# Weight matrices stored in DRAM block by block instead of as plain rows: a hybrid flow-matching step on one Trainium2 core

## The chip, the core and the metric

The kernel runs on one core of one Trainium2 chip. The metric is the device time of one execution in microseconds (us). Data live in DRAM (the chip's HBM) and are moved by the core's 16 DMA engines into the on-chip memory, SBUF, which has 128 partitions; matmul results land in PSUM. Five engines work side by side, each through its own instructions in a fixed order: TensorE (PE, whose weight loads are shown as PEld), VectorE (DVE), ScalarE (ACT), GpSimd (POOL) and SyncE (SP), which here only issues DMAs. An engine that meets an instruction whose semaphore has not come stands still, and with it all that is queued behind it.

## The reference, cut to what matters

One layer of a hybrid backbone is computed for 2048 latent tokens and 128 context tokens (2176 rows of 1024 channels, float32):

```python
xn   = rmsnorm(h, ln_g) * (1 + scale) + shift            # scale, shift, gate: silu(cond) @ w_ada + b_ada
proj = xn @ w_in                                         # (1024, 7696)
qkv, beta, dec, z_a, u_b, v_b, z_b, x_c, z_c, gates = split(proj)
o_a  = rmsnorm(delta_bidir(conv(qkv), decay, beta, state)) * silu(z_a)   # chunked gated DeltaNet, both directions
o_b  = chunk_sgu(u_b, v_b) * silu(z_b)                   # spatial gating in chunks of 128 tokens
o_c  = fourier_mix(x_c) * silu(z_c)
pb   = [o_a @ w_branch[0], o_b @ w_branch[1], o_c @ w_branch[2]]         # each (512, 1024)
merged = sum(sigmoid(gates[n]) * pb[n] for n in range(3))
y    = rmsnorm(h + gate * (merged @ w_out), final_g)     # w_out (1024, 1024)
```

The outputs are `y` for both token groups and the final DeltaNet states of the context tokens.

## The kernel before, in words

**Numbers.** Each float32 operand of a large product is split into two float16 parts, a high one (`hi`) and a low one (`lo`), scaled by a power of two; a product is three float16 matmuls, hi by hi, hi by lo and lo by hi. The normalised input is held whole in SBUF as `xh` and `xl`.

**Weights.** They come in blocks of 128 output columns. The list `wlist` (line 255) holds 84 entries in the order of use: 36 column blocks of `w_in` for the branches (4 for z_a, 12 for q, k and v of the DeltaNet, 4 for v_b, 16 for u_b, z_b, x_c and z_c), and then, for each branch in the order 1, 2, 0 and each of the 8 blocks of the merge, a block of `w_in` for the gate and a block of `w_branch`. The 8 blocks of `w_out` are read by `out_w` (line 1443) during the last merge. A block goes through these steps:

- `read_w` (line 198): SP issues one DMA into `wst`, a float32 tile with two buffers; contraction row k·128+p of the block goes to partition p, place k. So a partition gets 8 runs (4 for `w_branch`) of 128 floats, 512 bytes each, from rows that lie a whole matrix row apart in DRAM.
- `converting` (line 203): ACT squares the block and sums it (line 214, the square is written to the `lo` tile and thrown away), DVE makes the bound `wscb` (line 180), PE adds it over partitions, DVE takes from it the scale (lines 188 to 192), ACT writes `hi` (line 223), and DVE writes `lo` (line 224). That last step sets the `wst` buffer free for the next read.

`weight_step` does one of these steps at a time, called by `pace.tick` between the pieces of the main work, so that the conversion of coming weights is spread over it. The tiles' names tell the blocks apart: `zhi`/`zlo` for z_a, `v4hi`/`v4lo` for v_b, `bhi`/`blo` for `w_branch`, `wohi`/`wolo` for `w_out`, `whi`/`wlo` for the others.

**Stages.** First the modulation: 16 DMAs of `w_ada` into `ast`, matmuls and vector sums, results turned through `adr` (line 414). The first two weight blocks are read just behind the last `ast` load (line 437, `issue_after`). Then the input is normalised, and z_a, q, k and v are projected (the conv result is stored by POOL as `qkv`). From then on a generator, `delta()`, is woven into the main work in small steps: preparation of the DeltaNet's chunks, then the scan, 17 chunks forward and 17 backward, a chain of small matmuls with ACT and DVE steps between them (lines 908, 909, 980, 1002, 1019), its operands loaded by SP from DRAM (`skn`, `sv`, `sk`, `sq`, `sqk`, `sn`, `ES`, `N`). The main work beside it is the spatial gating, the Fourier mixing and then `merge` (line 1356), three times over 8 blocks: gate product, sigmoid, branch product with the operand `big` (read back through `st`, line 1351), their product added to a row `mrow`, which from the second pass on is loaded by SP (line 1371), added to by POOL and stored again by POOL's queue (`mrg`, line 1400). The last stage multiplies by `w_out`, adds the residual and normalises.

**Order.** The kernel is built with a scheduler that fixes each engine's order when the program is made. All loads named above, the weights' and the scan's, stand in SP's one queue (q1 in the profile), in that order; ACT issues some stores on its own queue (q10) and POOL on another (q0).

Of the kernel before, what the change touches and what calls it, by code (L numbers as in the profile page):

```python
# [20 lines left out]
P = 128  # L21
D = 1024
KT = 8
# [5 lines left out]
WB = 512  # L29
EPS = 1e-6  # L30
C_QKV, C_BD, C_ZA, C_U, C_V, C_ZB, C_XC, C_ZC, C_G = 0, 1536, 1552, 2064, 2576, 3088, 3600, 4112, 4624
# [25 lines left out]
def _const_array():  # L57
    i = np.arange(P)
    out = {}
    out["ident"] = np.eye(P)  # L60
    out["ones"] = np.ones((P, P))
    le = i[:, None] <= i[None, :]
    ge = i[:, None] >= i[None, :]
    out["tri_f"] = le * 1.0
    out["tri_b"] = ge * 1.0
    out["neg_f"] = np.where(le, 0.0, -3e4)
    out["neg_b"] = np.where(ge, 0.0, -3e4)
    b64, b32 = i // 64, i // 32
    a2 = np.arange(2)[None, :]
    out["m1f"] = (b32[:, None] == 2 * a2 + 1) * 1.0  # L70
    out["m1b"] = (b32[:, None] == 2 * a2) * 1.0
    out["m2f"] = (b64 == 1)[:, None] * 1.0
    out["m2b"] = (b64 == 0)[:, None] * 1.0
    out["bm"] = (b32[:, None] == np.arange(4)[None, :]) * 1.0
    c = np.arange(64)
    planes = [("c", 32) if (kd, k) == ("s", 0) else (kd, k) for q in range(0, 32, 8) for kd in "cs" for k in range(q, q + 8)]
    f = np.zeros((64, 64))
    for n_, (kind, k) in enumerate(planes):
        ang = 2 * np.pi * (c * k % 64) / 64
        f[:, n_] = (np.cos(ang) if kind == "c" else np.sin(ang)) / 8.0  # L80
    d2 = np.zeros((P, 2, 64))
    for r in range(2):
        d2[r * 64:(r + 1) * 64, r, :] = f
    out["dft2"] = d2.reshape(P, P)
    ang = 2 * np.pi * (i[:, None] * i[None, :] % P) / P
    C128, S128 = np.cos(ang) / math.sqrt(P), np.sin(ang) / math.sqrt(P)
    out["dftcs"] = np.concatenate([C128, S128], 1)
    out["dftms"] = -S128
    out["dfth"] = np.concatenate([C128[:, 0:65], S128[:, 1:64]], 1)
    r = np.arange(32)  # L90
    ang = 2 * np.pi * (r[:, None] * r[None, :] % 32) / 32
    C32, S32 = np.cos(ang) / math.sqrt(32), np.sin(ang) / math.sqrt(32)

    def bd(ms):
        m = np.zeros((P, P))
        for n_, x in enumerate(ms):
            m[n_ * 32:(n_ + 1) * 32, n_ * 32:(n_ + 1) * 32] = x
        return m

    out["rc"] = bd([C32] * 4)  # L100
    out["rms"] = bd([-S32] * 4)
    out["rmc"] = bd([-C32] * 4)
    out["rxa"] = bd([C32, -S32, -S32, -S32])
    out["rxb"] = bd([-S32, -C32, -C32, -C32])
    c32 = np.ascontiguousarray(np.concatenate([out[n_] for n_, _ in _CONSTS], 1).astype(np.float32))
    four = c32[:, _CF:] * np.float32(CS)
    hi = four.astype(np.float16)
    lo = (four - hi.astype(np.float32)).astype(np.float16)
    return np.ascontiguousarray(c32[:, 0:_CF]), np.ascontiguousarray(np.stack([hi, lo], 1))


class _W:
    pass


@with_exitstack
def hybrid_flow_kernel(ctx: ExitStack, tc: tile.TileContext, x_prompt, x_sample, state_delta, c, c_ctx, ln_g, w_ada,
                       b_ada, w_in, conv_w, a_log, dt_bias, o_norm_g, sgu_norm_g, w_spatial, b_spatial, w_branch,
                       w_out, final_g, consts, consts16, y_prompt, y_sample, new_state, dbg=None):
    nc = tc.nc  # L120
    V, A, G, PE, SY = nc.vector, nc.scalar, nc.gpsimd, nc.tensor, nc.sync
    uid, rot = [0], [0]
# [8 lines left out]
    def sb(pl, shape, tag, dt=F32, bufs=None):  # L131
        kw = {} if bufs is None else {"bufs": bufs}
        return pl.tile(list(shape), dt, tag=tag, name=nm(tag), **kw)
# [61 lines left out]
    def load_w(src, nkt, cols=P, hi=None, lo=None, tag="w", bufs=5):  # L195
        return convert(read_w(src, nkt, cols, tag), nkt, cols, hi, lo, tag, bufs)

    def read_w(src, nkt, cols=P, tag="w"):
        st = sb(wp, [P, nkt, cols], "wst" if cols == P else tag + "st", bufs=2 if cols == P else 1)
        SY.dma_start(st, src.rearrange("(k p) c -> p k c", p=P))  # L200
        return st

    def converting(w, st, nkt, cols=P, hi=None, lo=None, tag="w", bufs=5):
# [22 lines left out]
    def convert(st, nkt, *args, **kw):  # L226
        w = _W()
        for _ in converting(w, st, nkt, *args, **kw):
            pass
        return w  # L230
# [15 lines left out]
            mm(ps, lh[:, k, :], w.lo[:, k, c0:c0 + n], False, False)  # L246
            mm(ps, ll[:, k, :], w.hi[:, k, c0:c0 + n], False, k == nkt - 1)

    w_in_, w_ada_, b_ada_ = w_in[0], w_ada[0], b_ada[0]
    xs_, xp_ = x_sample[0], x_prompt[0]  # L250

    def xrows(t0, n):
        return xs_[t0:t0 + n, :] if t0 < NS else xp_[t0 - NS:t0 - NS + n, :]

    wlist = []
    for c0 in [C_ZA + g * P for g in range(4)]:
        wlist.append((w_in_[:, c0:c0 + P], KT, "z", 4))
    for c0 in ([C_QKV + i * P for i in range(12)] + [C_V + g * P for g in range(4)]
               + [x_ + g * P for g in range(4) for x_ in (C_U, C_ZB)] + [x_ + g * P for g in range(4) for x_ in (C_XC, C_ZC)]):
        wlist.append((w_in_[:, c0:c0 + P], KT, "v" if C_V <= c0 < C_V + WB else "w", 4))  # L260
    for n in (1, 2, 0):
        for db in range(KT):
            wlist.append((w_in_[:, C_G + n * D + db * P:C_G + n * D + (db + 1) * P], KT, "w", 4))
            wlist.append((w_branch[0, n][:, db * P:(db + 1) * P], 4, "b", 2))
    v4, vfilled = [], [0]
    goal = [0]
    wdone, wnext, wread, wlate, bwp, wsteps = [], [0], [], [0], [], []
# [1 line left out]
    def read_next():  # L269
        if len(wread) < min(len(wdone) - len(wsteps) + 2, len(wlist)):  # L270
            src, nkt, tag, bufs = wlist[len(wread)]
            wread.append(read_w(src, nkt))
# [26 lines left out]
    def getw(n=1, ahead=0):  # L299
        i = wnext[0]  # L300
        wnext[0] += n
        fetch(i + n)
        while len(wdone) - len(wsteps) < i + n:
            weight_step()
        fetch(i + n + ahead)
        r = wdone[i:i + n]
        return r[0] if n == 1 else r
# [84 lines left out]
    def load_x(t0, tn):  # L392
        xt = sb(p0p, [P, tn // P, D], "xt")
        SY.dma_start(xt, xrows(t0, tn).rearrange("(j p) d -> p j d", p=P))
        xts[t0] = xt

    for blk in range(8):
# [4 lines left out]
        for k0 in range(0, KT, 4):  # L402
            st = sb(p0p, [P, 4, 256], "ast", bufs=8)
# [31 lines left out]
    with tc.issue_after(last_ada.ins):  # L435
        read_next()
        read_next()
        load_x(*TBS[1])
        zaw = getw(4)
        bdp = sb(wp, [P, KT, 32], "bdp", F16, bufs=1)  # L440
        bdw = load_w(w_in_[:, C_BD:C_BD + 16], KT, 16, hi=bdp[:, :, 0:16], lo=bdp[:, :, 16:32], tag="d")
    szlate = []
    for ti, (t0, tn) in enumerate(TBS):
        if t0 not in xts:
            load_x(t0, tn)
        g = 0 if t0 < NS else 1
# [164 lines left out]
    for ct in range(12):  # L611
        w = getw(1, 2 if ct < 6 else min(4, 15 - ct))
# [292 lines left out]
    pair = lambda t_, h: (t_[:, 0, hs(h)], t_[:, 1, hs(h)])  # L905
# [301 lines left out]
    for g in range(4):  # L1207
# [5 lines left out]
        for ti, (t0, tn) in enumerate(TBS):  # L1213
            st = vrow[:, t0:t0 + tn]
# [224 lines left out]
    whi = sb(orp, [P, KT, D], "wohi", F16)  # L1439
    wlo = sb(orp, [P, KT, D], "wolo", F16)  # L1440
    winv = sb(orp, [P, KT], "winv8")

    def out_w(i):
        w = load_w(w_out[0][:, i * P:(i + 1) * P], KT, hi=whi[:, :, i * P:(i + 1) * P], lo=wlo[:, :, i * P:(i + 1) * P])
        V.tensor_mul(winv[:, i:i + 1], w.inv, sx)

    turn = []
# [42 lines left out]
    def tail(db):  # L1490
        out_w(db)
        if db == KT - 1:
            for _ in gates:
                pass
# [12 lines left out]
    for i_, t in enumerate(order):  # L1507
# [39 lines left out]
            SY.dma_start(out, hh)  # L1547


_INS = ['x_prompt', 'x_sample', 'state_delta', 'c', 'c_ctx', 'ln_g', 'w_ada', 'b_ada', 'w_in', 'conv_w', 'a_log',  # L1550
        'dt_bias', 'o_norm_g', 'sgu_norm_g', 'w_spatial', 'b_spatial', 'w_branch', 'w_out', 'final_g']
_OUTS = [((1, NP, D), 'float32'), ((1, NS, D), 'float32'), ((1, 1, 2, H, P, P), 'float32')]


# [21 lines left out]
```

## Time and profile before

| | |
|---|---|
| time, three runs | 2195.5, 2200.12, 2200.22 us; median 2200.12 |
| the profiled execution | 2197.38 us, its span 2195.6 us |
| granted TensorE clock, mean | 0.991 |
| busy: PE, PEld, DVE, ACT, POOL | 2122.4, 1218.2, 1311.2, 1013.1, 737.1 us |
| DMA queue q1 (SP) | 251690 packets, 267.38 MB, 40.5% of 16 engines' time |
| weight loads | 60 blocks of `w_in` of 512 KB, 24 of `w_branch` of 256 KB, 8 of `w_out` of 512 KB, one of 16 columns (`dst`) |

How to read it: the span is from the first to the last instruction, and 1.8 us of the profiled execution lie around it. Busy times of different engines overlap. An engine's row in a timeline ends in brackets with the time for which the engine stood idle before it and what ended that; an arrow in a group reads "written tile <- read tiles". "DMA share" is the mean busy share of the 16 DMA engines, and a packet is one contiguous run that one of them moves.

### The profile page before, as it was taken

To read this page: it belongs to the slowest core of one execution; us is meant where nothing else is said; L and a number is where in the kernel's file an instruction comes from. 1 tells how busy PE (TensorE), PEld (TensorE's weight loads), DVE (VectorE), ACT (ScalarE), POOL (GpSimd) and SP (SyncE) were. 2 spreads that over 40 slices of the span, in tenths; PEclk is the share of its full clock that TensorE was granted. 3 is DMA by queue.
4 is the path that set the end of the run, shared out by engine and by line. 5 is a ranking of instruction groups with operands and counts; after the bars stand their busy time and mean duration, and the time that the engine had idled before them with its cause. 6 is when DMAs were issued, how large, how long until landed. Compare 5 with 4: busy or idle time off the path is not lost.

```text
span 2195.6 us, 42626 instructions
## 1 busy us (share of the span) xinstructions
PE 2122.4 (97%) x16258; PEld 1218.2 (55%) x16258; DVE 1311.2 (60%) x3141; ACT 1013.1 (46%) x2345; POOL 737.1 (34%) x893
## 2 busy tenths in 40 slices
PE   7999999999999999899899999999999999999998
PEld 3565444455455577777455555555655444444444
DVE  5736845479878697466655555755574544233454
ACT  3544644355555674444544445655553422222332
POOL 1421533223334332443321223345442222122553
PEclk9999999999999999999999999999999999999999
DMA  8434733167777754434645556766665544333542
GB/s 282 143 96 146 266 114 110 61 208 219 239 224 238 213 167 107 119 118 143 217 155 166 167 161 187 239 195 206 204 200 154 166 125 129 119 101 109 183 151 106
DMA packets 304280, 365.11 MB, mean 166 GB/s; under 512 B 39393, under 2 KB 215754, under 8 KB 302026
## 3 DMA queue, kind: packets, MB, share of 16 engines
q1 hardware_dynamic: 251690, 267.38, 40.5%
q0 software_dynamic: 12688, 51.27, 6.5%
q10 hardware_dynamic: 39696, 43.72, 5.9%
q8 instruction: 128, 2.10, 0.4%
q14 instruction: 78, 0.64, 0.1%
HBM read 234.67 MB, written 127.62 MB: 165 GB/s over the span
## 4 chain that ended last, share of the span: by engine, by line
PE 45%; DVE 8%; DMA 7%; ACT 3%; issue 2%; POOL 1%; ACTq 0%; SPq 0%; POOLq 0%; DVEq 0%
PE b L166 45%; DMA st<-br 1%; DMA wst<-in_w_in_dram 1%; DVE XB L792 1%; DVE E L793 1%; DMA ei<-XB 1%; DMA wst<-in_w_branch_dram 1%; DMA sv<-kv 1%; DMA mt<-mrg 1%; DVE wlo L224 1%; DVE o L925 0%; DMA mrg<-mrow 0%; ACT nd L745 0%; DVE sv L980 0%; DVE big L1354 0%
## 5 line engine op out<-in xcount | busy, mean ns | idle before, releaser
L166 PE MATMUL b<-xh,whi 128*128 128x512 f16 (+1 forms) x1920 | 650.2, 347 | 7.4 <-DVE sg L1130 3.4
L166 PE MATMUL b<-xl,whi 128*128 128x512 f16 (+1 forms) x1920 | 650.6, 347 | 0.0
L166 PE MATMUL b<-xh,wlo 128*128 128x512 f16 (+1 forms) x1920 | 649.8, 347 | 0.0
L166 PEld LDWEIGHTS <-whi 128*128 128x128 f16 x3904 | 356.7, 98 | 339.6 <-issue 15.8
L166 PEld LDWEIGHTS <-wlo 128*128 128x128 f16 x1952 | 191.1, 98 | 177.9 <-issue 1.5
L166 PE MATMUL b<-big,bhi 128*128 128x512 f16 (+1 forms) x960 | 251.7, 348 | 5.8 <-ACT big L1353 5.4
L1393 POOL TENSOR_TENSOR mrow<-mrow,sg 128x512 f32<-128x512 f32 (+1 forms) x80 | 96.0, 1201 | 289.0 <-DVE sg L1392 158.5
L166 PE MATMUL b<-big,blo 128*128 128x512 f16 (+1 forms) x480 | 163.7, 348 | 0.0
L1383 ACT ACTIVATE sg<-b,winv 128x512 f32<-128x512 f32 (+1 forms) x120 | 74.1, 618 | 154.0 <-PE b L166 153.6
L166 PEld LDWEIGHTS <-xh 128*128 128x128 f16 x1496 | 118.7, 99 | 35.0 <-DVE yT L1306 3.9
L633 POOL TENSOR_TENSOR cy<-cy,raw 128x545 f32<-128x545 f32 (+1 forms) x48 | 76.6, 1623 | 180.3 <-ACT raw L632 180.3
L166 PEld LDWEIGHTS <-bhi 128*128 128x128 f16 x960 | 87.2, 98 | 77.0 <-ACT big L1353 1.6
L180 DVE CAST wscb<-wss 128x1 bf16<-128x1 f32 x93 | 14.3, 154 | 192.4 <-ACT wlo L214 79.4
L1392 DVE SCALAR_TENSOR_TENSOR sg<-b,binv,sg 128x512 f32<-128x512 f32 (+1 forms) x80 | 53.5, 668 | 101.2 <-PE b L166 91.1
L166 PE MATMUL b<-whi,xh 128*128 128x128 f16 x544 | 95.2, 222 | 5.2 <-DVE yT L1306 3.7
L166 PE MATMUL b<-wlo,xh 128*128 128x128 f16 x544 | 95.2, 222 | 0.0
L166 PE MATMUL b<-whi,xl 128*128 128x128 f16 x544 | 95.1, 222 | 0.0
L166 PE MATMUL b<-wohi,mh 128*128 128x512 f16 (+2 forms) x248 | 91.9, 372 | 1.5 <-ACT mh L1463 1.5
L865 POOL COPY T<-ES 32x256 f16<-32x256 f16 x68 | 28.7, 422 | 191.5 <-DMA ES<-ei 178.2
L166 PE MATMUL b<-wohi,ml 128*128 128x512 f16 (+2 forms) x248 | 91.7, 372 | 0.3 <-DVE ml L1464 0.3
L166 PE MATMUL b<-wolo,mh 128*128 128x512 f16 (+2 forms) x248 | 91.9, 372 | 0.0
L224 DVE SCALAR_TENSOR_TENSOR wlo<-wst,wsc,whi 128x1024 f16<-128x1024 f32 x52 | 72.6, 1399 | 31.2 <-ACT whi L223 30.4
(458 smaller groups left out, 4305.2 us busy)
## 6 DMA issues: line engine op xcount, KB each, us to landing
wst<-in_w_in_dram SPq DMA_DIRECT2D x60, 512.0 KB, 5.9
qkv<-cy POOLq DMA_DIRECT2D x12, 1089.0 KB, 5.2
st<-br SPq DMA_DIRECT2D x48, 256.0 KB, 4.5
mrow<-mrg SPq DMA_DIRECT2D x18, 512.0 KB, 3.5
mrow<-mrg SPq DMA_DIRECT2D x16, 576.0 KB, 3.8
mrg<-mrow POOLq DMA_DIRECT2D x16, 576.0 KB, 3.8
dc<-dec SPq DMA_DIRECT2D x17, 512.0 KB
kq<-qkv SPq DMA_DIRECT2D x34, 256.0 KB, 5.1
```

Source lines behind the costliest of these rows:

```text
L166: PE.matmul(out, l, r, start=start, stop=stop)
L180: V.tensor_copy(sb16, ss)
L224: V.scalar_tensor_tensor(w.lo, st, s, w.hi, ALU.mult, ALU.subtract)
L633: G.tensor_tensor(y[:, c0:c1], y[:, c0:c1], raw[:, 1 + c0:1 + c1], ALU.mult)
L792: V.tensor_tensor(t3, X3[:, 0:k, k:k + 1].to_broadcast([P, k, n_]), E3[:, k:k + 1, k:32].to_broadcast([P, k, n_]), ALU.mult)
L793: V.tensor_tensor(E3[:, 0:k, k:32], E3[:, 0:k, k:32], t3, ALU.subtract)
L865: G.tensor_copy(T16[rows(a0, b), :, :, b], ES[0:32, :, 2 * a0 + b, :, wT])
L1383: A.activation(sg, ps, AF.Sigmoid, scale=gw.inv)
L1392: V.scalar_tensor_tensor(sg, ps, binv[:, 1:2], sg, ALU.mult, ALU.mult)
L1393: G.tensor_tensor(mr, mr, sg, ALU.add)
```

## The change

The weights are laid out anew before the launch, on the host: for each block of 128 columns, partition p's 8 (or 4) runs of 128 floats stand side by side, and the blocks stand one behind the other. A block is then 128 rows of 4 KB (2 KB for `w_branch`), 512 KB (256 KB) in one piece; the 16 columns for beta and decay become 128 rows of 512 bytes. The kernel reads each block with one DMA as before, of the same size, into the same tile. Nothing else in the kernel's text is changed.

```diff
+def _by_block(w, starts, width=P):
+    w = np.asarray(w)
+    return np.ascontiguousarray(np.stack([w[:, c0:c0 + width].reshape(-1, P, width).transpose(1, 0, 2).reshape(P, -1) for c0 in starts]))
+
+def _laid_out(inputs):
+    w_in, w_branch, w_out = [np.asarray(inputs[n_])[0] for n_ in ("w_in", "w_branch", "w_out")]
+    cols = [db * P for db in range(KT)]
+    return {
+        "w_blk": _by_block(w_in, [c0 + i * P for c0, i in _blocks()]),
+        "w_bd": _by_block(w_in, [C_BD], 16)[0],
+        "w_brb": np.stack([_by_block(w_branch[n], cols) for n in range(3)]),
+        "w_outb": _by_block(w_out, cols),
+    }
...
     def read_w(src, nkt, cols=P, tag="w"):
         st = sb(wp, [P, nkt, cols], "wst" if cols == P else tag + "st", bufs=2 if cols == P else 1)
-        SY.dma_start(st, src.rearrange("(k p) c -> p k c", p=P))
+        SY.dma_start(st, src.rearrange("p (k c) -> p k c", c=cols))
         return st
...
-    for c0 in [C_ZA + g * P for g in range(4)]:
-        wlist.append((w_in_[:, c0:c0 + P], KT, "z", 4))
...
-    for n in (1, 2, 0):
-        for db in range(KT):
-            wlist.append((w_in_[:, C_G + n * D + db * P:C_G + n * D + (db + 1) * P], KT, "w", 4))
-            wlist.append((w_branch[0, n][:, db * P:(db + 1) * P], 4, "b", 2))
+    for i, (n_, g) in enumerate(_blocks()):
+        wlist.append((w_blk[i], KT, "z" if n_ == C_ZA else "v" if n_ == C_V else "w", 4))
+        if n_ >= C_G:
+            wlist.append((w_brb[(n_ - C_G) // D, g], 4, "b", 2))
...
-        w = load_w(w_out[0][:, i * P:(i + 1) * P], KT, hi=whi[:, :, i * P:(i + 1) * P], lo=wlo[:, :, i * P:(i + 1) * P])
+        w = load_w(w_outb[i], KT, hi=whi[:, :, i * P:(i + 1) * P], lo=wlo[:, :, i * P:(i + 1) * P])
```

`_blocks()` lists the 60 blocks of `w_in` in the order of `wlist`. The load of the 16 columns reads `w_bd` in the same way.

More of the change, by code (lines that the diff above doesn't have):

```diff
@@ L109, in _const_array, with _blocks @@
     return np.ascontiguousarray(c32[:, 0:_CF]), np.ascontiguousarray(np.stack([hi, lo], 1))
+def _blocks():
+    parts = [(C_ZA, g) for g in range(4)] + [(C_QKV, i) for i in range(12)] + [(C_V, g) for g in range(4)]
+    for pair in ((C_U, C_ZB), (C_XC, C_ZC)):
+        parts += [(x_, g) for g in range(4) for x_ in pair]
+    return parts + [(C_G + n * D, db) for n in (1, 2, 0) for db in range(KT)]
+def _by_block(w, starts, width=P):
[10 more added lines that the diff above has]
+    }
 class _W:
@@ L117, in hybrid_flow_kernel @@
 def hybrid_flow_kernel(ctx: ExitStack, tc: tile.TileContext, x_prompt, x_sample, state_delta, c, c_ctx, ln_g, w_ada,
-                       b_ada, w_in, conv_w, a_log, dt_bias, o_norm_g, sgu_norm_g, w_spatial, b_spatial, w_branch,
-                       w_out, final_g, consts, consts16, y_prompt, y_sample, new_state, dbg=None):
+                       b_ada, w_blk, w_bd, conv_w, a_log, dt_bias, o_norm_g, sgu_norm_g, w_spatial, b_spatial, w_brb,
+                       w_outb, final_g, consts, consts16, y_prompt, y_sample, new_state, dbg=None):
     nc = tc.nc
@@ L247, in gemm_N @@
             mm(ps, ll[:, k, :], w.hi[:, k, c0:c0 + n], False, k == nkt - 1)
-    w_in_, w_ada_, b_ada_ = w_in[0], w_ada[0], b_ada[0]
+    w_ada_, b_ada_ = w_ada[0], b_ada[0]
     xs_, xp_ = x_sample[0], x_prompt[0]
@@ L255, in hybrid_flow_kernel @@
     wlist = []
-    for c0 in [C_ZA + g * P for g in range(4)]:
-        wlist.append((w_in_[:, c0:c0 + P], KT, "z", 4))
-    for c0 in ([C_QKV + i * P for i in range(12)] + [C_V + g * P for g in range(4)]
-               + [x_ + g * P for g in range(4) for x_ in (C_U, C_ZB)] + [x_ + g * P for g in range(4) for x_ in (C_XC, C_ZC)]):
-        wlist.append((w_in_[:, c0:c0 + P], KT, "v" if C_V <= c0 < C_V + WB else "w", 4))
-    for n in (1, 2, 0):
-        for db in range(KT):
-            wlist.append((w_in_[:, C_G + n * D + db * P:C_G + n * D + (db + 1) * P], KT, "w", 4))
-            wlist.append((w_branch[0, n][:, db * P:(db + 1) * P], 4, "b", 2))
+    for i, (n_, g) in enumerate(_blocks()):
+        wlist.append((w_blk[i], KT, "z" if n_ == C_ZA else "v" if n_ == C_V else "w", 4))
+        if n_ >= C_G:
+            wlist.append((w_brb[(n_ - C_G) // D, g], 4, "b", 2))
     v4, vfilled = [], [0]
@@ L440, in hybrid_flow_kernel @@
         bdp = sb(wp, [P, KT, 32], "bdp", F16, bufs=1)
-        bdw = load_w(w_in_[:, C_BD:C_BD + 16], KT, 16, hi=bdp[:, :, 0:16], lo=bdp[:, :, 16:32], tag="d")
+        bdw = load_w(w_bd, KT, 16, hi=bdp[:, :, 0:16], lo=bdp[:, :, 16:32], tag="d")
     szlate = []
@@ L1547, in hybrid_flow_kernel @@
             SY.dma_start(out, hh)
-_INS = ['x_prompt', 'x_sample', 'state_delta', 'c', 'c_ctx', 'ln_g', 'w_ada', 'b_ada', 'w_in', 'conv_w', 'a_log',
-        'dt_bias', 'o_norm_g', 'sgu_norm_g', 'w_spatial', 'b_spatial', 'w_branch', 'w_out', 'final_g']
+_INS = ['x_prompt', 'x_sample', 'state_delta', 'c', 'c_ctx', 'ln_g', 'w_ada', 'b_ada', 'w_blk', 'w_bd', 'conv_w', 'a_log',
+        'dt_bias', 'o_norm_g', 'sgu_norm_g', 'w_spatial', 'b_spatial', 'w_brb', 'w_outb', 'final_g']
 _OUTS = [((1, NP, D), 'float32'), ((1, NS, D), 'float32'), ((1, 1, 2, H, P, P), 'float32')]
@@ L1563 @@
     arrays, args = {}, []
-    fixed = dict(zip(("consts", "consts16"), _const_array()))
+    fixed = dict(zip(("consts", "consts16"), _const_array()), **_laid_out(inputs))
     for name in _INS + ["consts", "consts16"]:
```

## The prediction, written before the changed kernel was run

> **What bounds the kernel now.** I read the page first, for who is busy and what chain ended last.
>
> ```profile
> PE 2122.4 (97%) x16258; PEld 1218.2 (55%) x16258; DVE 1311.2 (60%) x3141; ACT 1013.1 (46%) x2345; POOL 737.1 (34%) x893
> DMA packets 304280, 365.11 MB, mean 166 GB/s; under 512 B 39393, under 2 KB 215754, under 8 KB 302026
> PE b L166 45%; DMA st<-br 1%; DMA wst<-in_w_in_dram 1%; DVE XB L792 1%; DVE E L793 1%; DMA ei<-XB 1%; DMA wst<-in_w_branch_dram 1%; DMA sv<-kv 1%; DMA mt<-mrg 1%; DVE wlo L224 1%; DVE o L925 0%; DMA mrg<-mrow 0%; ACT nd L745 0%; DVE sv L980 0%; DVE big L1354 0%
> ```
>
> TensorE is busy for 2122.4 of 2195.6 us, so nothing that speeds up a transfer can bring more than the 73.2 us in which it stands, and most of these have other causes. Weight loads hold two places of about 1% in the chain. Next the waits, since a load matters only where an engine stands for it:
>
> ```profile
> ACT blo L214 <- DMA wst<-in_w_branch_dram: 72.2, 22, 7.6
> ACT wlo L214 <- DMA wst<-in_w_in_dram: 65.7, 25, 7.2
> ACT wolo L214 <- DMA wst<-in_w_out_dram: 18.8, 8, 3.7
> ```
>
> ACT stands 156.7 us in all before the squaring of a block that has not landed (columns: total, times, longest). TensorE itself never waits for a weight load by name. So a late block costs something only by way of ACT: whatever is queued on ACT behind the squaring, the scan's `S`, `u`, `v` at line 908 above all, comes late, and where the scan's chain is what TensorE needs next, TensorE stands.
>
> **What the change does to the program.** The built programs have the same instructions in the same order on all five engines, with the same waits; only the 93 weight loads carry another access pattern. So no engine work is added, moved or removed, and no wait. All that can differ is when these loads land and what they do to other transfers on the 16 DMA engines. If a 4 KB row is one packet, 68 loads of 1024 packets become 128 each, 24 of 512 become 128, and `dst` 1024 become 128: 304280 packets become about 233,200.
>
> **What one load costs.** The list of issues gives medians from issue to landing:
>
> ```profile
> wst<-in_w_in_dram SPq DMA_DIRECT2D x60, 512.0 KB, 5.9
> mrow<-mrg SPq DMA_DIRECT2D x18, 512.0 KB, 3.5
> sv<-kv SPq DMA_DIRECT2D x34, 256.0 KB, 2.9
> xr<-in_x_sample_dram SPq DMA_DIRECT2D x16, 512.0 KB, 3.2
> wst<-in_w_branch_dram SPq DMA_DIRECT2D x24, 256.0 KB, 3.3
> ```
>
> `mrow` and `xr` are 512 KB loads in runs of 4 KB; `sv` is 256 KB in runs of 2 KB. Read plainly, a block of `w_in` would land 5.9 - 3.4 = 2.5 us sooner and one of `w_branch` 3.3 - 2.9 = 0.4 us. But such a median also holds the time spent behind other loads of the queue. So I looked at stretches in which one load alone is moved, two of `w_in` and two of `xr`; packets, MB and the share of 16 engines follow the queue's name.
>
> ```profile
> q1 hardware_dynamic: 1040, 0.52, 77.6%
> ```
>
> ```profile
> q1 hardware_dynamic: 1040, 0.52, 53.5%
> ```
>
> ```profile
> q1 hardware_dynamic: 144, 0.52, 73.9%
> ```
>
> ```profile
> q1 hardware_dynamic: 144, 0.52, 73.0%
> ```
>
> The stretches are 366.3 to 368.8, 332.7 to 336.2, 2038.5 to 2040.5 and 2068.9 to 2071.1 us. The engines work 0.776 x 2.5 = 1.94 and 0.535 x 3.5 = 1.87 us for 512 KB in 512 byte packets, and 0.739 x 2.0 = 1.48 and 0.730 x 2.2 = 1.61 us in 4 KB packets (the 16 packets over are the completions). On the means that is 1.90 - 1.54 = 0.36 us less. For `w_branch` and for two 2 KB-run loads that overlap (152 packets, 0.28 MB):
>
> ```profile
> q1 hardware_dynamic: 528, 0.26, 22.2%
> ```
>
> ```profile
> q1 hardware_dynamic: 152, 0.28, 66.5%
> ```
>
> These stretches are 1958 to 1962 and 1400.9 to 1402.4 us: 0.89 and 1.00 us. So 2 KB runs gain nothing that I can see, and I price `w_branch` at 0, with 0.4 as the far end.
>
> Here the Trainium skill says otherwise: DMA: Bandwidth & Descriptors, Specifications, gives 512 bytes as the smallest transfer that runs at line rate. By it the sum below would be nought. The trace does not agree, at 1.90 against 1.54 us, but it agrees for `w_branch`.
>
> So the price of a `w_in` or `w_out` load lies between 0.36 us (the engines' own time) and 2.5 us (the landing medians). I take the low end and a little: the transfers' own time is what the change surely takes off, and the waits behind other loads stay.
>
> **Where it lies on the path.** The chain of waits has exactly these pieces of weight loads, and one load that was issued behind a weight load (start, us):
>
> ```profile
> 1052.68 3.98 DMA wst<-in_w_branch_dram
> ...
> 1070.05 5.42 DMA sn<-n
> ...
> 1215.09 5.75 DMA wst<-in_w_in_dram
> ...
> 1433.48 6.99 DMA wst<-in_w_in_dram
> ...
> 1501.42 6.60 DMA wst<-in_w_branch_dram
> ...
> 1547.47 3.01 DMA wst<-in_w_branch_dram
> ...
> 1567.57 6.92 DMA wst<-in_w_in_dram
> ```
>
> In the timeline of TensorE these are the gaps that follow (in brackets), which cap what can be won there:
>
> ```profile
> 1076.27 0.38 PE L166 MATMUL b<-big,bhi 128*128 128x512 f16 x1 [1.68 <-ACT big L1353]
> ...
> 1222.87 0.28 PE L166 MATMUL b<-v,R 128*128 128x128 f16 x2 [0.55 <-ACT R L880]
> ...
> 1444.30 0.77 PE L166 MATMUL b<-u,kn 128*128 128x128 f16 x11 [1.21 <-DVE u L909]
> ...
> 1576.23 0.22 PE L166 MATMUL b<-u,kn 128*128 128x128 f16 x1 [1.78 <-ACT u L908]
> ```
>
> At the start the chain is not followed, so I read the timelines of ACT, DVE and PE:
>
> ```profile
> 40.10 1.06 ACT L214 ACTIVATE zlo<-wst 128x1024 f16<-128x1024 f32 x1 [0.52 <-DMA wst<-in_w_in_dram]
> ...
> 53.32 1.06 ACT L214 ACTIVATE zlo<-wst 128x1024 f16<-128x1024 f32 x1 [0.66 <-DMA wst<-in_w_in_dram]
> ```
>
> ```profile
> 41.28 0.16 DVE L180 CAST wscb<-wss 128x1 bf16<-128x1 f32 x1 [1.51 <-ACT zlo L214]
> 41.35 0.73 DVE L414 COPY adr<-b 2x256 f32<-2x256 f32 x2
> ```
>
> ```profile
> 39.87 0.59 PE L166 MATMUL b<-ast,scT 128*2 128x256 f32 x2
> 41.80 0.28 PE L416 MATMUL b<-cst,adr 2*128 2x2 f32 x2 [1.34 <-DVE adr L414]
> ```
>
> On DVE the modulation's `adr` stands behind `wscb` of the second block, though its matmuls ended at 40.46. Both first blocks come one behind the other, so the second lands two prices sooner: up to 41.35 - 40.46 = 0.89 us of the start go.
>
> **The sum.** At 0.36 us: the start 2 x 0.36 = 0.7; the third block at 53.32, 0.4; the three `w_in` pieces of the chain 3 x 0.36 = 1.1; `sn` behind a block 0.4; `w_branch` 0. That is 2.6 us. At 2.5 us, each capped by its gap: 0.89 + 0.66 + 0.55 + 1.21 + 1.78 + 1.68, and 3 x 0.4 for `w_branch`, together 8.0 us. Between 64 and 737 us the chain is not followed; no wait of TensorE there names a weight, and I count nothing. The other loads lie beside TensorE's work: from 1690 to 2000 us, where the blocks for the last merge and `w_out` come,
>
> ```profile
> 1690.00:2000.00 310.00, 310.00 (x1726) 151.21 (x1725) 122.58 (x326) 88.73 (x143) 66.34 (x66) 1.00 0.41 126
> ```
>
> TensorE is busy for 310.00 of 310 us, and hides them; were it to stand there, each would be worth its 0.36 us. I take 3.5 us, nearer to the low end. From the profiled execution's 2197.38 us that is 2193.9; this execution lies 2.7 us under the median of the three runs, 2200.12, and the forecast for the median is 2196.5 us. A measurement of this kernel can tell about 0.3%, 6.6 us, from no change: 2193.5 to 2206.7.
>
> **The rivals.**
>
> *Faster, by the landing time.* The crowded loads are the ones on the path: 5.75, 6.99 and 6.92 us. If short rows, not the crowd, make them long, the 8.0 us above are due, and ACT's 156.7 us of standing fall by 2.5 / 5.9 of 84.5 (`w_in`, `w_out`) and 0.4 / 3.3 of 72.2 (`w_branch`), 45 us. If a quarter of that comes to the scan's chain, 11 us: about 2189 us. For it speaks that the loads of 4 KB rows have medians of 3.2 and 3.5 us; against it, that loads moved alone show 0.36 us.
>
> *Slower, by turns at the DMA engines.* In the second merge pass SP's load of `mrow` waits until POOL's store of the row before it has landed, and the scan's loads stand behind it in SP's queue. The chain shows this once, and SP's own timeline shows what waits:
>
> ```profile
> 1590.56 3.93 DMA mrg<-mrow
> 1594.95 6.00 DMA sv<-kv
> ```
>
> ```profile
> 1594.54 0.32 SPq L1371 DMA_DIRECT2D mrow<-mrg  x1
> 1594.95 0.38 SPq L949 DMA_DIRECT2D sv<-kv  x1
> ```
>
> A store has 8 packets for each engine. If queues take turns packet by packet, 8 turns of a 512 byte weight packet (1.90 / 64 = 0.03 us) hold it up by 0.24 us, and 8 turns of a 4 KB one by 1.54 us, 1.3 us more; of a 2 KB one by 0.9 - 0.24, 0.65 us more. With 8 blocks of each sort in the pass: 8 x 1.3 + 8 x 0.65 = 15.6 us, less the 3.5: about 2212 us. It decides from some 10 us on, when nearly every `w_in` block meets a store whose landing SP then waits for. Against it: one such piece in the whole chain. That each engine goes round its queues packet by packet is what the Trainium skill states (DMA: Bandwidth & Descriptors, Queues, rings and completion order); no row here shows it.
>
> *Nothing.* If crowded loads are bound by the crowd alone, the gain is below 1 us: 2199 to 2200. It has the forecast's sign and verdict, and I count it in.
>
> **How the numbers follow.** The forecast with "nothing": 0.46, which is the chance of within 0.3%. The landing rival: 0.40, all of it faster by more. The turns: 0.14, slower by more. The range takes in 2189 with its own spread below and the milder half of the slower case: 2183 to 2207; the likeliest case alone spans 2192 to 2200.
>
> **What would show it.** In the profile after: a `w_in` load alone at 128 packets and about 1.54 us of the engines' time; about 233,200 packets in all; ACT's standing for `wst` 156.7 us before and 135 to 150 after (110 by the landing rival); `adr` up to 0.9 us sooner at the start; TensorE's busy time unchanged and its standing some 3 us less. The forecast is wrong if the gaps at 1222, 1444 and 1576 us go altogether (then the landing rival holds), or if SP's `mrow` loads wait longer for `mrg` stores and TensorE's standing grows between 1340 and 1690 us (then the turns).

## The result, and the profile after

The changed kernel takes 2191.0 us (median of 8, 2187.96 to 2196.42) against 2199.39 us for the kernel before on the same chip (2194.8 to 2204.93): ratio 0.9959, 95% interval 0.9946 to 0.9973, faster by 0.41%. Two repeats, on two chips, gave 0.9973 and 0.9952. The forecast was 2196.5 in a range of 2183 to 2207. The range holds the time and the sign is right, but the forecast gain is less than half of what came: its sum was 3.5 us, the medians are 8.4 us apart, and the time lies below the likeliest case's own range of 2192 to 2200, near the 2189 of the landing rival. The stated range held it only because it was stretched to take that rival in. By the 0.3% that was set as the bound it is faster, which the forecast held a little less likely than no change (0.40 against 0.46).

The profiled execution of the changed kernel took 2196.42 us with a span of 2194.6, the longest of its eight. So its span lies only 1.0 us below that of before, and the places have to be read one by one. First the profile's own page: engines, packets, the SP queue (packets, MB, share of 16 engines' span).

```profile
PE 2125.6 (97%) x16258; PEld 1220.6 (56%) x16258; DVE 1311.4 (60%) x3141; ACT 1014.4 (46%) x2345; POOL 734.8 (33%) x893
...
DMA packets 233240, 365.11 MB, mean 166 GB/s; under 512 B 38369, under 2 KB 132938, under 8 KB 230986
...
q1 hardware_dynamic: 180650, 267.38, 39.3%
```

The instruction counts are those of before, the bytes too, and 71,040 packets are gone. ACT's waits for the blocks:

```profile
ACT blo L241 <- DMA wst<-in_w_brb_dram: 65.8, 22, 6.9
ACT wlo L241 <- DMA wst<-in_w_blk_dram: 54.5, 24, 6.8
...
ACT wolo L241 <- DMA wst<-in_w_outb_dram: 12.1, 8, 3.1
```

Together 132.4 us for 156.7. (These three rows are not all of it: with `zlo` and `v4lo` ACT stood 185.6 us before, where the prediction says "156.7 us in all", and 157.3 us now.) The issues, with the medians from issue to landing:

```profile
wst<-in_w_blk_dram SPq DMA_DIRECT2D x60, 512.0 KB, 5.2
mrow<-mrg SPq DMA_DIRECT2D x18, 512.0 KB, 3.6
...
wst<-in_w_brb_dram SPq DMA_DIRECT2D x24, 256.0 KB, 2.9
```

A `w_in` block lands 0.7 us sooner (5.2 for 5.9) and a `w_branch` block 0.4 (2.9 for 3.3; in the repeats 3.0 and 3.1). One load alone, in the transfers from 361.5 to 364.2, 858.2 to 860.6 (both `w_in`) and 1957.2 to 1959.3 us (`w_branch`):

```profile
q1 hardware_dynamic: 144, 0.52, 59.5%
...
q1 hardware_dynamic: 144, 0.52, 66.1%
...
q1 hardware_dynamic: 144, 0.26, 47.3%
```

That is 128 packets and 16 completions, and 0.595 x 2.7 = 1.61 and 0.661 x 2.4 = 1.59 us of the engines for a `w_in` block where it was 1.90; and 0.473 x 2.1 = 0.99 for `w_branch`, where it was 0.89. Now the chain of waits, the pieces of weight loads at the places that the prediction named (the first, at 1065.76, ends ahead of the gap at 1073, where `sn` stood before):

```profile
1065.76 5.20 DMA wst<-in_w_blk_dram
...
1212.52 5.85 DMA wst<-in_w_blk_dram
...
1433.79 6.10 DMA wst<-in_w_blk_dram
...
1500.53 6.37 DMA wst<-in_w_brb_dram
...
1566.46 4.93 DMA wst<-in_w_blk_dram
```

and TensorE's timeline at the same instructions, and at the start DVE's:

```profile
41.13 0.28 PE L438 MATMUL b<-cst,adr 2*128 2x2 f32 x2 [0.37 <-DVE adr L436]
...
1073.37 0.38 PE L193 MATMUL b<-big,bhi 128*128 128x512 f16 x1 [0.53 <-ACT big L1375]
...
1220.40 0.28 PE L193 MATMUL b<-v,R 128*128 128x128 f16 x2 [0.66 <-ACT R L902]
...
1443.72 0.77 PE L193 MATMUL b<-u,kn 128*128 128x128 f16 x11 [0.32 <-DVE u L931]
```

```profile
40.60 0.16 DVE L207 CAST wscb<-wss 128x1 bf16<-128x1 f32 x1 [1.12 <-ACT zlo L241]
40.67 0.73 DVE L436 COPY adr<-b 2x256 f32<-2x256 f32 x2
```

The start is 0.67 us earlier (41.13 for 41.80), because `adr`, which stands behind `wscb` on DVE, begins 0.68 us sooner (40.67 for 41.35). The gap of 1.78 us that was at 1576.23 has no row any more. What took its place is read on ACT, before and after:

```profile
1574.51 1.06 ACT L214 ACTIVATE wlo<-wst 128x1024 f16<-128x1024 f32 x1 [5.09 <-DMA wst<-in_w_in_dram]
...
1575.57 0.61 ACT L908 ACTIVATE u<-sv 128x512 f16<-128x512 f32 x1
```

```profile
1571.41 1.06 ACT L241 ACTIVATE wlo<-wst 128x1024 f16<-128x1024 f32 x1 [3.09 <-DMA wst<-in_w_blk_dram]
...
1572.46 0.61 ACT L930 ACTIVATE u<-sv 128x512 f16<-128x512 f32 x1
```

The load was issued 1.1 us earlier and took 4.93 us for 6.92, so the squaring and the `u` behind it come 3.1 us sooner; TensorE, 1.1 us earlier too, finds `u` ready. Among the other gaps, the one at 1073 is 0.53 us here for 1.68, but 1.87 and 1.60 in the two repeats below, and the one at 1443 is 0.32 for 1.21, but 0.43 and 1.74 there: only the gap at 1576 stays away.

### The profile page after: what moved, and what is told of

Same layout as the page of the kernel before. It is cut to its first block, busy times and chain, and to the rows that moved or that the text cites. A ratio compares the mean times of both kernels' runs of the same rounds, so it can differ in the third digit from the quotient of the medians.

```text
span 2194.6 us, 42626 instructions
## 1 busy us (share of the span) xinstructions
PE 2125.6 (97%) x16258; PEld 1220.6 (56%) x16258; DVE 1311.4 (60%) x3141; ACT 1014.4 (46%) x2345; POOL 734.8 (33%) x893
## 2 busy tenths in 40 slices
DMA packets 233240, 365.11 MB, mean 166 GB/s; under 512 B 38369, under 2 KB 132938, under 8 KB 230986
## 4 chain that ended last, share of the span: by engine, by line
PE 46%; DVE 7%; DMA 6%; ACT 3%; issue 2%; POOL 1%; ACTq 0%; SPq 0%; POOLq 0%; DVEq 0%
PE b L193 46%; DMA st<-br 1%; DMA wst<-in_w_blk_dram 1%; DVE XB L814 1%; DVE E L815 1%; DMA ei<-XB 1%; DMA wst<-in_w_brb_dram 1%; DVE big L1376 1%; DVE wlo L251 0%; DMA ES<-ei 0%; ACT nd L767 0%; ACT big L1375 0%; DVE sv L1002 0%; DMA of<-sz 0%; DVE o L947 0%
```

## Experiments

**The change again, and the kernel before again.** Since the one profile of after was of a long execution, the change ran twice more, and the kernel before was profiled a second time.

> The changed kernel once more, as the measure for the parts. Every theory: ratio to before 0.996, some 8 us (6 to 12). A second profile of it shows how far two executions of one program lie apart: if TensorE's half-clock stretches fall elsewhere than in the first profile (20.5 us lost there against 17.1 in before, without the last one), the span differs by up to some 4 us while the order of work is the same.

Measured: 2190.51 us against 2197.46, ratio 0.9973 (0.9964 to 0.9983); span 2194.2; ACT's standing for `wst` 133.1 us.

> The change unchanged, a third time, beside the version that also stores the 24 pieces of `w_ada` in rows of 4 KB. Two comparisons gave 0.9959 and 0.9973 of the kernel before. If the gain is a fixed sum of about 6 to 8 us, the ratio is again between 0.9955 and 0.9980 and the median near 2190.5 us; a ratio above 0.9985 would say that most of it was wander of single executions. ACT's standing for a free `wst` is expected at 131 to 135 us (132.4 and 133.1 in the two profiles so far, 156.7 before).

Measured: 2189.47 us (2187.06 to 2193.76) against 2200.39, ratio 0.9952 (0.9938 to 0.9966), just beyond the 0.9955 expected; span 2192.0; ACT's standing 132.2 us.

> The kernel before once more, for a second profile. If single executions of one kernel wander by where TensorE's clock is halved after a stand, the same instruction of the two profiles of before is up to 2 or 3 us apart between 400 and 2000 us, while the first 62 us agree within 0.3 us; ACT's standing for a free `wst` stays at 155 to 159 us (156.7 in the first). If the profiles of before agree within 0.5 us all along, the differences of 1 to 3 us between kernels in mid-course are the kernels' own.

Measured: 2200.29 us, span 2198.5. The two profiles of before agree within 0.45 us up to 62 us (0.3 was expected), and are then 2.3 us apart from 272 us on, 0.6 at 985 and up to 4.9 near 1410. ACT's standing was 164.8 us, outside the 155 to 159 expected. So one profile of before is good to 2 to 5 us in mid-course and to 8 us of ACT's standing. The second profile also shows what the first did not:

```profile
274.53 0.39 PE L166 MATMUL b<-xh,wlo 128*128 128x512 f16 x1 [1.35 <-DVE wlo L224]
...
1581.01 0.22 PE L166 MATMUL b<-u,kn 128*128 128x128 f16 x1 [1.75 <-ACT u L908]
```

Here TensorE does stand for a weight's `lo` part, 1.35 us at 274.53 (and 0.53 us at 250.92), and the stand for `u` that was at 1576 is there again. The stand at 274.53 is not one for a late load: ACT squared this block at 258.93, 14 us before its `wlo` step, which stands on DVE behind a clearing of `XB` that began at 271.41 for 268.15 in the first profile:

```profile
258.93 1.06 ACT L214 ACTIVATE wlo<-wst 128x1024 f16<-128x1024 f32 x1 [0.39 <-DMA wst<-in_w_in_dram]
```

```profile
271.41 0.91 DVE L778 MEMSET XB<- 128x1024 f32 x1 [4.39 <-ACT whi L223]
...
273.31 1.16 DVE L224 SCALAR_TENSOR_TENSOR wlo<-wst,wsc,whi 128x1024 f16<-128x1024 f32 x1
```

Three other kernels below with short rows there (the merge alone, `w_branch` alone, the first four blocks alone) stand 0 us between 64 and 460. So it isn't shown that the change takes this stand away. In the three profiles of the changed kernel TensorE stands 0, 0 and 0.07 us between 64 and 460 us, and 0, 0.13 and 0 us at the instruction of 1576. The load ahead of the stand for `u`, in the chains of the second before, and of the second and third after:

```profile
1572.46 6.80 DMA wst<-in_w_in_dram
```

```profile
1566.92 5.27 DMA wst<-in_w_blk_dram
```

```profile
1567.10 5.07 DMA wst<-in_w_blk_dram
```

It takes 6.92 and 6.80 us in 512 byte packets, and 4.93, 5.27 and 5.07 in 4 KB ones: 1.8 us less. The kernels below that change a part, or more, narrow this. In the chains of `w_branch` alone and of the first four blocks alone, both with short rows at this place, and of the change with `w_ada`, with long ones, the load reads:

```profile
1568.93 5.57 DMA wst<-in_w_bd_dram
```

```profile
1563.37 6.24 DMA wst<-in_w_bd_dram
```

```profile
1557.90 5.74 DMA wst<-in_w_blk_dram
```

Over all profiles it takes 5.57 to 6.92 us with short rows in the old place (five, mean 6.4) and 4.93 to 5.74 with long ones (six in whose chain it stands, mean 5.2), and TensorE's stand behind it is 1.78, 1.75, 1.16, 1.61 and 0.42 us against 0, 0.13, 0, 0, 0, 0 and 0.59: some 1.2 us less on the means, and on each of the three chips with profiles of both the short rows stand longer. At 1433 it is 6.99 and 6.51 against 6.10, 6.22 and 7.64, and at 1213 it is 5.75 and 6.38 against 5.85, 5.80 and 5.52: 0.1 and 0.3 us less on the means. So one of the three places paid 1.2 us, half of the landing rival's price, and the two others hardly any.

The stage in which the second merge pass runs, 1340 to 1690 us (columns: TensorE busy, weight loads, DVE, ACT, POOL, granted clock, DMA share, GB/s), in before and its repeat, then in the changed kernel and its two repeats:

```profile
1340.00:1690.00 350.00, 338.78 (x2965) 201.77 (x2964) 214.47 (x560) 194.13 (x545) 152.64 (x181) 1.00 0.65 198
```

```profile
1340.00:1690.00 350.00, 340.90 (x2976) 202.63 (x2974) 215.41 (x566) 194.88 (x548) 151.28 (x182) 1.00 0.65 200
```

```profile
1340.00:1690.00 350.00, 341.09 (x2951) 202.71 (x2949) 214.72 (x567) 194.09 (x543) 151.66 (x182) 1.00 0.63 197
```

```profile
1340.00:1690.00 350.00, 343.35 (x2980) 204.10 (x2978) 216.81 (x571) 195.47 (x548) 153.59 (x182) 1.00 0.64 199
```

```profile
1340.00:1690.00 350.00, 342.84 (x2978) 203.91 (x2975) 216.18 (x570) 195.14 (x546) 152.47 (x183) 1.00 0.64 200
```

TensorE stands 11.2 and 9.1 us of this stage before, 8.9, 6.7 and 7.2 after: 2.6 us less on the means. The other kernels bear it out: with long `w_in` rows in the merge 5.7 to 8.0 us (four profiles), with short ones in the old place 8.6 to 9.4 (three). With `w_in` alone it is 6.5 and with `w_branch` alone 8.6, so it comes from the `w_in` blocks.

**The place alone, with the short rows.** The blocks are stored one behind the other, but each in rows of 512 bytes, so that a load is 1024 packets as before, out of 512 KB in one piece instead of rows 30,784 bytes apart.

```
-    ... w[:, c0:c0 + width].reshape(-1, P, width).transpose(1, 0, 2).reshape(P, -1) ...
+    ... w[:, c0:c0 + width].reshape(-1, P, width) ...
-        SY.dma_start(st, src.rearrange("p (k c) -> p k c", c=cols))
+        SY.dma_start(st, src.rearrange("k p c -> p k c"))
```

> Each block lies in one piece in DRAM as in the change, but with contraction block k outermost, so that a partition still gets 8 (4) runs of 512 bytes: 1024 packets for a load, as before. Own-time theory (short runs cost the DMA engines 1.90 us for 512 KB against 1.54): no gain, ratio 0.999 to 1.001, and a load alone still needs 1.85 to 1.95 us of the engines. Place theory (rows of a 30 KB pitch are slow to read in DRAM, one piece is fast): the whole gain, ratio 0.996, and a load alone needs about 1.5 us.

Measured: 2194.64 us against 2197.46, ratio 0.9986 (0.9978 to 0.9995), some 3 us. ACT's waits, and one `w_in` load alone (362.2 to 365.0 us):

```profile
ACT wlo L241 <- DMA wst<-in_w_blk_dram: 66.3, 25, 7.5
ACT blo L241 <- DMA wst<-in_w_brb_dram: 64.8, 21, 7.0
ACT wolo L241 <- DMA wst<-in_w_outb_dram: 16.5, 8, 3.7
```

```profile
q1 hardware_dynamic: 1040, 0.52, 62.8%
```

0.628 x 2.8 = 1.76 us of the engines with 1040 packets, between 1.90 and 1.60. So about half of the engines' price comes from where the rows lie, half from their length, and neither of the two expectations holds alone. In the stage from 1340 to 1690 us TensorE stands 7.1 us in this kernel, as little as with long rows, and 0.56 us for `u` at 1576. ACT's standing (147.6 us) falls by a third to a half of what it falls by in the change. The Trainium skill (DMA: Bandwidth & Descriptors, Why small descriptors are slow (HBM only)) puts some 3 cycles on each packet beside one for each 32 bytes; by an estimate from it a block in 512 byte packets takes 19/16 over 131/128 = 1.16 times as long as in 4 KB ones. The trace agrees nearly, 1.76 over 1.60 = 1.10, once the place is the same.

**The parts by stage.** Of the 60 blocks of `w_in`, the 36 ahead of the merge, or the 24 of the gates with `w_branch` and `w_out`, are stored in long rows; the rest are read from the tensors as they are.

```
-        wlist.append((w_blk[i], ...
+        wlist.append((w_blk[i] if i < 36 else w_bd[:, n_ + g * P:n_ + (g + 1) * P], ...   # or i >= 36
```

(`w_bd` is the whole of `w_in` in these kernels.)

> Only the 36 blocks of w_in used before the merge come in 4 KB rows; all others as before. Own-time theory, by the prediction's places: the start's three loads, about 1.1 us, and little else, since the chain names no weight between 64 and 1052 us: 1 to 2 us, ratio 0.9990 to 0.9996. If the gain comes from loads that no chain names (in the preparation of the DeltaNet chunks, 350 to 940 us), 4 us or more, ratio below 0.998.

Measured: 2195.32 us against 2197.46, ratio 0.9995 (0.9984 to 1.0005): at most 3.5 us.

> The other way round: the 24 gate blocks of w_in, all of w_branch and w_out in long rows, the 36 blocks before the merge as before. Own-time theory by the prediction's places: 1.1 us of the three chain pieces and 0.4 of sn, 1.5 to 2.5 us, ratio 0.9990. Landing theory (a crowded load gains far more than its own time): 5 us or more, ratio 0.9977 or less, and ACT's waits for wst of w_in shorter by 1 us each.

Measured: 2192.47 us against 2197.46, ratio 0.998 (0.9969 to 0.9991): 2 to 7 us, between the two expectations. ACT at the instruction of 1574.51, in the first and in the second of the two:

```profile
1572.78 1.06 ACT L244 ACTIVATE wlo<-wst 128x1024 f16<-128x1024 f32 x1 [4.92 <-DMA wst<-in_w_bd_dram]
```

```profile
1571.44 1.06 ACT L244 ACTIVATE wlo<-wst 128x1024 f16<-128x1024 f32 x1 [3.07 <-DMA wst<-in_w_blk_dram]
```

and TensorE in the first:

```profile
1574.50 0.22 PE L193 MATMUL b<-u,kn 128*128 128x128 f16 x1 [1.61 <-ACT u L933]
```

With short rows in the merge the stand for `u` is 1.61 us; with long rows there alone it is gone. The load in the chain of the first of the two:

```profile
1566.45 6.30 DMA wst<-in_w_bd_dram
```

That is the change's work at this place, and shown by both halves. The two ratios add up to 1.1 + 4.4 = 5.5 us of 2198, where the whole change on the same chip has 0.0027, 5.9 us.

**The parts by tensor.** `w_in` alone, `w_branch` alone, and of `w_in` the first four blocks alone.

```
-        "w_brb": np.stack([_by_block(w_branch[n], cols) for n in range(3)]),
-        "w_outb": _by_block(w_out, cols),
+        "w_brb": np.ascontiguousarray(w_branch),
+        "w_outb": np.ascontiguousarray(w_out),
```

> The 60 blocks of w_in (and the 16 columns) in long rows; w_branch and w_out as before. If w_branch gains nothing, as the prediction had it, this is the whole gain but for w_out: 6 to 7 us, ratio 0.997. If each w_branch block lands 0.4 us sooner because 128 rows are fewer to start than 512, the three w_branch pieces of the chain are missing here: 4 to 5 us, ratio 0.998.

Measured: 2193.03 us against 2197.59, ratio 0.9974 (0.9962 to 0.9986), 5.7 us, between the two expectations and unable to tell them apart.

> Only the 24 blocks of w_branch in rows of 2 KB, all else as before. Prediction's price: nought, ratio 0.9995 to 1.0005. Landing price of 0.4 us a block: 1.2 us of the chain's three pieces, up to 3 us with loads behind them, ratio 0.9986 to 0.9995, and ACT's standing for these blocks 72 us in before, 64 to 68 here.

Measured: 2196.11 us against 2197.59, ratio 0.9992 (0.998 to 1.0003): inconclusive, 1.8 us by its middle. The median from issue to landing of a `w_branch` load is 3.2 or 3.3 us in the six profiles with its short rows and 2.9 to 3.1 in the seven with its long ones: some 0.2 us less, although the engines' own time for it is no less (0.99 us for 0.89 above). ACT's standing for these blocks, 66.8 us here and 72.2 before, is as the landing price expected, but it is 64.4 us in the kernel with long rows ahead of the merge alone, which leaves `w_branch` as it was; so it decides nothing.

> Only the first four blocks of w_in (z_a) in long rows. Prediction: adr at 41.4 us comes 0.7 to 0.9 us sooner and the third block at 53.3 another 0.4 us; TensorE is packed from 64 us on, so some 1.1 us stay: ratio 0.9995, just about what can be told from 1. If the start's gain is lost again at the next stand of TensorE (578, 661 us), nought. If a start that lies 1 us elsewhere shifts where the half-clock stretches fall, up to 3 us either way.

Measured: 2195.27 us against 2197.59, ratio 0.9989 (0.9975 to 1.0003): inconclusive by the time. By the profile the start is 1.2 us earlier at 46 us and 1.7 at 62 us, no less than the whole change brings there (0.7 to 0.9, and 1.2 to 1.4). With long rows ahead of the merge alone it is 0.4 and 0.9 us. In the kernel with short rows ahead of the merge the same instructions are 0.1 and 0.4 us earlier, and with `w_branch` alone 0.4 and 0.1 us later. So the start's gain is that of the first blocks.

**A further version: `w_ada` in long rows too.** At the start TensorE stands for pieces of `w_ada` (16 of its 24 loads of 512 KB, in rows of 1 KB), 3.6 to 5.2 us in the profiles of before and of the change. Each of the 24 is stored as 128 rows of 4 KB.

```
+        "w_ada": np.ascontiguousarray(w_ada.reshape(2, 4, P, 12, 256).transpose(3, 0, 2, 1, 4).reshape(12, 2, P, 1024)),
-            last_ada = SY.dma_start(st, w_ada_[k0 * P:(k0 + 4) * P, blk * 256:(blk + 1) * 256].rearrange("(k p) c -> p k c", p=P))
+            last_ada = SY.dma_start(st, w_ada_[blk, k0 // 4].rearrange("p (k c) -> p k c", k=4))
```

> The changed kernel, and also w_ada stored as 24 pieces of 128 rows of 4 KB in place of runs of 1 KB: 16 loads at the start, where the DMA engines are busy for 0.92 to 0.98 of the time, and 8 beside the last merge. Own-time theory: 512 KB in 1 KB runs of a 12 KB pitch cost the engines some 1.65 us against 1.55, so 16 x 0.1 = 1.6 us sooner at the last of them; place theory the same or a little more, 16 x 0.2 = 3 us. So 1 to 3 us under the changed kernel, ratio to before 0.9955 to 0.9968.

Measured: 2188.75 us against 2197.59, ratio 0.9959 (0.9943 to 0.9975).

> The change and `w_ada` as 24 pieces of 128 rows of 4 KB, on the same chip as the change alone. If the 24 loads ahead of the first matmuls set the end by their landing, the start is 2 us earlier (the instruction at 41 to 42 us of the other kernels about 2 us sooner than in the change alone) and the time 1.5 to 2.5 us below that of the change alone. If what is gained at the start is given back later, at a wait that does not depend on the start, the two agree within 0.5 us.

Measured, on the same chip as the third run of the change: 2186.72 us against 2189.47 for the change and 2200.39 for before, ratio to before 0.9942 (0.9926 to 0.9957). The start, in the change and in this version:

```profile
41.16 0.28 PE L438 MATMUL b<-cst,adr 2*128 2x2 f32 x2 [0.37 <-DVE adr L436]
```

```profile
39.11 0.28 PE L440 MATMUL b<-cst,adr 2*128 2x2 f32 x2
```

2.05 us earlier, as expected, and 2.75 us less in the medians, a little over the 1.5 to 2.5 expected. The intervals of the two ratios overlap; what speaks for it is that the start's 2 us are seen in both of its profiles. Whether all of it lasts to the end can't be read from single profiles: at 2150 us the two of this version are 7.6 and 12.5 us ahead of the first profile of before and those of the change 1.0, 1.4 and 3.6, but those of `w_in` alone and of the first four blocks alone are 5.5 and 4.7 us ahead. It has the lowest median of these kernels.

## Why the prediction was right, and where its sizes were not

- **What the change does to the program**: right. The order and the counts are unchanged, and the packets are 233,240 for "about 233,200".
- **ACT as the way in**: right, and its size just missed. The forecast had 135 to 150 us of standing in the three rows, the landing rival 110; it is 132.4, 133.1 and 132.2 against 156.7 and 164.8.
- **The start**: right. 0.7 + 0.4 = 1.1 us was the term; it measured 1.2 to 1.4 at 62 us, `adr` 0.68 of the 0.9 that could go.
- **The price of a load** failed in "The sum", where it was taken as "the low end and a little". A `w_in` load alone has the predicted 1.6 us of the engines' time, but by the records of the packets its last one ends 2.84 us after its issue for 3.30 (medians of the seven loads after and the two before that nothing else overlapped): 0.46, not 0.36, and the first packet starts sooner too (0.97 for 1.04). Among other traffic it varies by place: 0.1 to 0.3 us at 1213 and 1433, 1.2 us at 1566. The landing rival's 2.5 us for each is not there, so that the time came near its 2189 is in part luck; but at 1576 TensorE won 1.2 us on the means, and up to the cap of 1.78, where the sum had 0.36. The 0.9 us by which the forecast's 3.5 goes beyond its sum of 2.6 were taken from no row.
- **`w_branch` at 0** failed in part. The reasoning went by the engines' own time, which indeed does not fall; the load lands some 0.2 us sooner all the same, half of its far end of 0.4. Whether the kernel gains by it is not shown (1.8 us, inconclusive). The Trainium skill (DMA: Bandwidth & Descriptors, Specifications) gives 512 bytes as the smallest transfer at line rate; the engines' time of this load agrees with that, that of a `w_in` load does not.
- **"Between 64 and 737 us ... I count nothing"** failed in part. The first profile of before shows no wait for a weight there and the second 1.88 us, which is not shown to be a load's doing. But between 480 and 504 us the seven profiles with long rows in the `w_in` blocks ahead of the merge gain 0.9 to 1.6 us on the first profile of before, and the five with short rows in the old place 0 to 0.8. So on the means 1 us goes with the `w_in` rows there; no wait of TensorE there is over 0.33 us or names a weight, so by which path stays open.
- **TensorE's standing "some 3 us less", busy time unchanged**: span less busy time is 73.2 and 75.8 us before, 69.0, 70.7 and 68.9 after: 5.0 less on the means. This can't be read as the change's gain, because it is 63.3 to 69.3 us in the other kernels, and as low as 64.9 with the first four blocks alone. Busy time is 2122.4 and 2122.75 before, 2125.6, 2123.5 and 2123.1 after, by the clock (below).
- **The turns** did not come, by either of their signs. SP's standing for `mrg` ahead of the `mrow` loads is 80.9 and 79.4 us before and 75.4, 76.2 and 75.1 after, and TensorE's standing from 1340 to 1690 us fell by 2.6 us. The `mrow` loads of 512 KB do land later once issued (3.5 and 3.7 us before, 3.6, 4.3 and 4.3 after), but it is 4.1 with the first four blocks alone, whose merge is as before. That one row is one turn of the engines, on which the rival's price stands, no run shows.
- **"Nothing"** is ruled out by three intervals whose upper ends are 0.9966 to 0.9983; and no part of the change measured slower than before.

Added up from the profiles: 1.3 us at the start, some 1 between 480 and 504, and 2.4 to 2.6 in the stage from 1340 to 1690, 1.2 of it at 1576. That is 4.7 to 4.9 us of the 7.0 to 10.9 by which the medians differ. The three profiled executions of the changed kernel lie 4.3 to 5.5 us above their medians, and TensorE's standing between 1020 and 1120 us alone is anywhere from 9.1 to 13.2 us over all profiles, so the profiles can't show the rest, and where it comes from is not settled.

## What to carry to other kernels

Price a faster load by when its last packet lands at each place where an engine stands for it, not by the DMA engines' time alone: here a load priced at 0.36 us was worth 0.1 at one place and some 1.2 at another, and one with no price at all landed 0.2 us sooner. Before a gap is put down to a change, look at more profiles, of the same kernel and of kernels that change a part: the gap at 1576 was 1.8 us in two executions and 0.4 in another with the same rows there, and a stand of 1.35 us for a weight came in one of five. And lay out each tile as one piece with a partition's data in one run; nothing that was stored so here made the kernel slower, and the gain of the loads ahead of the first work is the easiest to see in the profiles.

## What the runs showed that was not expected

TensorE's granted clock falls to 0.5 for 3.41 us, or two or three times that, after some of its stands, and which stands are followed by it differs between executions. After the stand for `mh` ahead of the output, in after and in before:

```profile
2008.83 0.39 PE L193 MATMUL b<-wohi,mh 128*128 128x512 f16 x1 [2.07 <-ACT mh L1485]
2010.15 0.55 PE L193 MATMUL b<-wohi,ml 128*128 128x512 f16 x1 [0.28 <-DVE ml L1486]
```

```profile
2011.07 0.39 PE L166 MATMUL b<-wohi,mh 128*128 128x512 f16 x1 [1.51 <-ACT mh L1463]
2012.39 0.39 PE L166 MATMUL b<-wohi,ml 128*128 128x512 f16 x1 [0.28 <-DVE ml L1464]
```

In after the second matmul takes 0.55 us, at half clock, and by 2015 us 1.7 of the 2.2 us are lost by which the output was ahead. Counted as half of these stretches, without the one at the end, the half clock costs at most 17.1 and 18.8 us in the two profiles of before, 20.5, 18.8 and 18.8 in the three of the change, and 17.1 and 13.7 in the two with `w_ada`. Without it the spans are 2178.5 and 2179.7 before, 2174.1, 2175.4 and 2173.2 after, 4.9 us less on the means; but they are 2170.4 to 2175.7 in the five kernels with a part of the change, and lowest with the first four blocks alone, so taking the clock out does not put the kernels in order either. The Trainium skill (TensorE: Matmul & The Clock Gate, Part 1: The HAM clock gate (the "warmup" mystery)) says that the clock is set by how busy the array was in a window of some 3.4 us that runs freely, so that the cost varies from run to run; the trace agrees, in stretches of 3.41 us.
